# Four more seven-product pairs in three early groups of a hybrid attention and convolution block, and a later first one in the output product

## The chip, the cores and the metric

The kernel runs on one NeuronCore of a Trainium2 chip. The metric is the device time of one execution in microseconds. The engines are named as the profile names them: PE (TensorE, the matmuls), PEld (its weight loads), DVE (VectorE), ACT (ScalarE), POOL (GpSimd) and SP (SyncE, which issues the transfers).

## The reference, cut to what matters

One layer on 256 rows of 4096 numbers, everything in float32 (sizes: T = 256, D = 4096, the attention and the convolution half 2048 each):

```python
xn   = rms_norm(x, norm_in_g)
proj = xn @ w_in                       # 4096 x 14336
q, k, v, z_a, a_c, g_c, z_c = split(proj, 2048 each)
y_a  = rms_norm(chunked_attention(q, k, v), attn_out_g) * silu(z_a)
u    = a_c * sigmoid(g_c)              # "glu"
u    = causal_depthwise_conv(u, 31 taps) + b_dw
u    = silu(layer_norm(u))
y_c  = rms_norm(u @ w_pw + b_pw, conv_out_g) * silu(z_c)
h    = x + concat(y_a, y_c) @ w_out    # 4096 x 4096
gate = sigmoid(rms_norm(h) @ w_ple_gate + b)
h    = h + gate * (p @ w_ple)
out  = rms_norm(h, final_g)
```

## The kernel before, in words

**Products in float32.** A float32 matrix is split into a high part (a cast by ACT, L203, tiles `wh` for weights and `uh` for sums of weights) and a low part (the difference, by DVE, L204, `wl` and `ul`). One product of a 128x128 block of activations with 128x512 weights is then three matmuls: high by high, low by high, high by low. All matmuls of the large products are issued in `add`, L367; `product`, for v alone, issues at L217.

**Groups.** `mixed_product` makes one group: two blocks of 512 columns for two halves of 128 rows, in four accumulator banks of PSUM. It runs over the 32 blocks of the contraction in 16 pairs. A plain pair is 8 block products, 24 matmuls. A pair marked with a star in the order lists (`units("1 3 5 7 0* ...")`) is made as one step of Strassen's method with seven block products, 21 matmuls. For it DVE adds weights first (`ua`, L423 and L424; `ub`, L427 and L428), which are split too (two `uh` casts, two `ul` differences), and only half of the first weight tile is split. It uses four more banks, the helpers P1, P5, P6 and P7, which come from the pool `ps_tmp` of four banks that attention, transposes and the layer norm use as well, and which are read out behind the last seven-product pair of a group (`helper_sums`, L465 to L468). It also needs four combinations of the pair's blocks of activations: differences and sums with a high and a low part (`combine_again` and `combined_parts`, L279, L256 to L259 and, for the low part, L265). For x they lie in `xS`; there are combinations for the pairs 0, 2, 4 and 6, and so only these can be starred in the groups that read x early. Later the kernel has room for all even pairs.

**The order of the groups**, with the start of each group's matmuls in the profiled execution: glu(0) 6 us, glu(1) 99, q and k of heads(0) 186, its v 272, glu(2) 317, heads(1) 408 and v 496, glu(3) 542, heads(2) 633 and v, heads(3) 766 and v 859, the pointwise product 905, four gated z groups 999, four w_out groups 1328, the gate of the per-layer inputs 1666 to 2004. The attention of the heads of one call runs inside the next group: attention(1) in glu(3), attention(2) in heads(3).

**Work in between.** What isn't a product waits in a queue `later`: the 31 taps of the convolution (L666, L670), combinations, and, in heads(3), the layer norm: sums over channels, the mean as a matmul (L728), centring (L740), squares (L744, L748), variance, spread. `fill` takes a few from it behind each pair, four in these groups. A scheduler then sets the order of every engine's instructions; DVE, ACT and PE each run theirs strictly in that order. The mean matmul takes a bank of `ps_tmp`, so it stands behind the read of the first helper.

**Buffers.** Weights come by transfers of 512 KB on SP's queue into five tiles `wt`; `wh` and `wl` have three tiles each, `ua`/`ub` two, `uh`/`ul` two, the activation pool `act` eight places (for x while it is read, the outputs of attention and of the convolution).

The order lists concerned are `early` (glu(1) to glu(3) and all heads), `late` (the first w_out group and the first gate group) and `dense` (most later groups).

Of the kernel before, what the change touches and what calls it, by code (L numbers as in the profile page):

```python
# [16 lines left out]
P = 128  # L17
# [8 lines left out]
def hybrid_block(  # L26
# [285 lines left out]
    def units(text):  # L312

        return [(int(u.rstrip("*")), u.endswith("*")) for u in text.split()]


    dense = units("1 0* 3 2* 5 4* 6* 7 8* 9 10* 11 12* 14* 13 15")
    delayed = units("1 3 5 7 0* 9 2* 11 4* 13 6* 15 8* 10 12 14")
    first = units("0 1 3 5 7 9 11 13 15 2* 8 4* 10 6* 12 14")
    early = units("1 3 5 7 0* 9 2* 11 4* 13 6* 15 8 10 12 14")  # L320
    final = units("1 0* 3 2* 5 4* 6* 7 8* 9 10* 12* 11 13 14 15")
    late = units("1 3 5 7 9 11 13 15 0* 2 4* 6 8* 10* 12 14")

    def mixed_product(
        w, col, lhs, comb, order, on_helpers, ahead=None, fills=(0,), on_begin=None, apart=NB,
# [66 lines left out]
        for n, (pair, seven) in enumerate(order):  # L392
            if n < done:
                continue
            if ahead:
                ahead(pair)
            wts = []
            for k in range(2):
                wt = wpool.tile([P, 2, NB], F32, tag="w", name="wt")
                nc.sync.dma_start(wt, two_columns(w, 2 * pair + k, col, apart))  # L400
                wts.append(wt)
            if n >= len(order) - n_left:
                for k in range(2):
                    tiles = left[2 * (n - len(order) + n_left) + k]
                    held.append((2 * pair + k, parts_of(wts[k], 2, tiles and tiles())[0]))
                fill(fills[n % len(fills)])
                continue
            if not seven:
                for k in range(2):
                    add_plain(n, k, *parts_of(wts[k], 2)[0])  # L410
                fill(fills[n % len(fills)])
                continue
            begins = not helper
            if begins:
                for name in ("P1", "P5", "P7", "P6"):
                    helper[name] = ps_tmp.tile([P, NB], F32, tag="tmp", name=f"acc_{name}")
                banks.update(helper)
            w0, w1 = wts
            ua = upool.tile([P, 2, NB], F32, tag="u", name="ua")
            ub = upool.tile([P, 2, NB], F32, tag="u", name="ub")  # L420
            plus = partial(nc.vector.tensor_tensor, op=ALU.add)
            w0h, w0l = parts_of(w0, 1)[0]
            plus(ua[:, 0], w0[:, 0], w0[:, 1])  # L423
            plus(ua[:, 1], w0[:, 1], w1[:, 1])  # L424
            uah, ual = pair_parts(ua)
            w1h, w1l = parts_of(w1, 2)[0]
            plus(ub[:, 0], ua[:, 0], w1[:, 1])  # L427
            plus(ub[:, 1], ub[:, 0], w1[:, 0])  # L428
            ubh, ubl = pair_parts(ub)
            first = len(made)  # L430

            def s_of(i):
                t, at = comb[pair // 4], pair % 4
# [72 lines left out]
    ssq_x = cpool.tile([P, NH, D // NB], F32, name="ssq_x")  # L506
    xT = []

    xS = [big_tile(upool) for _ in range(2)]
    r_x = cpool.tile([P, NH], F32, name="r_x")  # L510

    def combinations(c, then=lambda ins: None):

        rest = []

        def begin():
            rows = spool.tile([P, 2, NB], F32, tag="stage", name="comb")
            rest.append(
                combine_again(
                    xS[c // 2], 2 * (c % 2), xT[c], 0, (rows[:, 0], rows[:, 1]), then  # L520
                )
            )

        return begin, lambda: rest.pop()()
# [150 lines left out]
    def glu_conv(c):  # L675
        if c == 0:
            sg, gate = scaled_pair(
                w_in0, o_a, o_g - o_a, first, r_x, (1,), begin=first_pairs
            )
        else:  # L680
            sg, gate = scaled_pair(w_in0, o_a + c * NB, o_g - o_a, early, r_x, (4,))
        for h in range(NH):
            nc.scalar.activation(gate[:, h, :], gate[:, h, :], AF.Sigmoid)
            tt(sg[:, h, :], sg[:, h, :], gate[:, h, :], ALU.mult)
        uT = spool.tile([P, 4, T], F32, tag="hd", name="uT", bufs=5)
        for pair in range(2):
# [178 lines left out]
    def heads(g):  # L865
# [9 lines left out]
            ),  # L875
        )
        nc.gpsimd.memset(bias[: P // 2, :, : P // 2], NEG)
        q, k = scaled_pair(w_in0, o_q + g * NB, o_k - o_q, early, r_x, (4,))
        qT, kT = to_heads(q, "qT"), to_heads(k, "kT")
        if g == n_g - 1:  # L880
            first_sums.close()
# [111 lines left out]
    for c0 in range(0, D // NB, 2):  # L993
# [8 lines left out]
        def on_helpers(helper):  # L1002
# [6 lines left out]
            tt(h11, h11, z[1][1], ALU.subtract)  # L1009

        acc = mixed_product(
            w_out[0], c0 * NB, yT, yS, dense if c0 else late, on_helpers,
            ahead=y_ahead if c0 == 0 else before_last(h_ahead) if c0 + 2 == D // NB else None,
            fills=(2,),
        )
# [203 lines left out]
```

## Time and profile before

| | |
|---|---|
| runs | 2042.84, 2042.05, 2042.83 us, median 2042.83 |
| profiled execution | 2042.15 us, of it 2040.4 span |
| PE busy | 2022.8 us, 99% of the span |
| DVE busy | 1879.8 us, 92% |
| ACT busy | 1177.1 us, 58% |
| granted clock | 0.998 |
| transfers | 412 MB, 202 GB/s |

The span runs from the first to the last instruction. "Busy" counts instructions of the engine itself. In a line of waits stand the waiting engine, the tile and line that waited, what ended the wait, and the total, the count and the longest in us. In a timeline stand start and duration in us, then the instruction with its shape; an "x3" row runs from the first one's start to the last one's end.

### The profile page before, as it was taken

How to read it: one execution, taken by the hardware profiler on the slowest of the kernel's cores; microseconds unless marked ns; L12 is line 12 of the kernel's file. 1: busy time of each engine (PE TensorE's matmuls, PEld its weight loads, DVE VectorE, ACT ScalarE, POOL GpSimd, SP SyncE). 2: the span in 40 equal slices, each digit the busy share in tenths (PEclk: the TensorE clock that was granted, in tenths of full speed). 3: DMA queues.
4: the chain of work that ended last, by engine and by line, in shares of the span. 5: the costliest groups of instructions: out<-in, count | busy, mean ns of one | idle time of the engine just before them, and what ended most of it. 6: DMA issues, size and time to landing. Idle time of an engine off the chain costs nothing.

```text
span 2040.4 us, 25991 instructions
## 1 busy us (share of the span) xinstructions
PE 2022.8 (99%) x9118; PEld 1662.6 (81%) x9118; DVE 1879.8 (92%) x2675; ACT 1177.1 (58%) x1517; POOL 15.7 (1%) x19
## 2 busy tenths in 40 slices
PE   9999999999999999999999999999999999999997
PEld 7888888887888788888888888888888888888876
DVE  7999999899877998866999999999999999999997
ACT  7655535554464536565566556676565666655555
POOL 0000000000000000000100000000000000000000
PEclk9999999999999999999999999999999999999999
DMA  8666665666566665555666666676666656666765
GB/s 290 191 196 207 196 197 165 205 190 194 175 196 200 194 187 184 182 189 196 198 209 204 196 216 201 221 231 207 212 204 200 215 185 207 197 223 205 233 209 176
DMA packets 161852, 412.28 MB, mean 202 GB/s; under 512 B 12974, under 2 KB 16190, under 8 KB 161722
## 3 DMA queue, kind: packets, MB, share of 16 engines
q1 hardware_dynamic: 161072, 409.80, 63.4%
q8 instruction: 71, 1.16, 0.2%
q10 hardware_dynamic: 650, 0.84, 0.1%
q14 instruction: 59, 0.48, 0.1%
HBM read 406.39 MB, written 4.19 MB: 201 GB/s over the span
## 4 chain that ended last, share of the span: by engine, by line
PE 91%; DVE 6%; issue 2%; ACT 0%; DMA 0%; POOLq 0%; POOL 0%; ACTq 0%; DVEq 0%
PE acc L367 64%; PE acc_P L367 15%; PE acc L217 9%; DVE wl L204 2%; DVE cv L670 2%; PE tmp_ps L169 1%; DVE ul L204 1%; PE tmp_ps L831 0%; PE tmp_ps L849 0%; PE tmp_ps L816 0%; DMA wt<-in_w_ple_dram 0%; PE tmp_ps L124 0%; PE tmp_ps L854 0%; PE tmp_ps L855 0%; PE tmp_ps L856 0%
## 5 line engine op out<-in xcount | busy, mean ns | idle before, releaser
L367 PE MATMUL acc<-wh,big_t 128*128 128x512 f32 x3874 | 1200.0, 392 | 0.0
L203 ACT CAST wh<-wt 128x1024 fp32r<-128x1024 f32 (+1 forms) x737 | 717.2, 982 | 584.4 <-PE acc L367 364.8
L204 DVE TENSOR_TENSOR wl<-wt,wh 128x1024 fp32r<-128x1024 f32 (+1 forms) x737 | 826.3, 1132 | 76.0 <-ACT wh L203 71.8
L367 PEld LDWEIGHTS acc<-wh,big_t 128*128 128x128 f32 x3874 | 724.9, 188 | 149.6 <-ACT big_t L155 0.6
L367 PE MATMUL acc<-wl,big_t 128*128 128x512 f32 x1937 | 746.6, 391 | 1.2 <-DVE wl L204 1.2
L367 PEld LDWEIGHTS acc<-wl,big_t 128*128 128x128 f32 x1937 | 363.1, 188 | 80.0 <-DVE wl L204 5.2
L670 DVE SCALAR_TENSOR_TENSOR cv<-uT,dw,cv 128x255 f32<-128x255 f32 (+25 forms) x480 | 203.5, 461 | 0.9
L203 ACT CAST uh<-ub 128x1024 fp32r<-128x1024 f32 x118 | 124.1, 1052 | 119.5 <-DVE ub L428 101.3
L367 PE MATMUL acc_P<-uh,big_t 128*128 128x512 f32 x594 | 181.4, 391 | 0.0
L217 PE MATMUL acc<-wh,big_t 128*128 128x512 f32 x560 | 173.3, 390 | 0.0
L203 ACT CAST uh<-ua 128x1024 fp32r<-128x1024 f32 x118 | 124.3, 1053 | 68.1 <-DVE ua L424 62.4
L204 DVE TENSOR_TENSOR ul<-ub,uh 128x1024 fp32r<-128x1024 f32 x118 | 143.8, 1219 | 8.2 <-ACT uh L203 7.6
L204 DVE TENSOR_TENSOR ul<-ua,uh 128x1024 fp32r<-128x1024 f32 x118 | 143.7, 1218 | 0.2
L367 PEld LDWEIGHTS acc_P<-uh,big_t 128*128 128x128 f32 x594 | 110.2, 188 | 25.8 <-ACT uh L203 3.8
L217 PEld LDWEIGHTS acc<-wh,big_t 128*128 128x128 f32 x560 | 105.0, 188 | 21.5
L367 PE MATMUL acc_P<-ul,big_t 128*128 128x512 f32 x297 | 113.9, 393 | 1.1 <-DVE ul L204 1.1
L217 PE MATMUL acc<-wl,big_t 128*128 128x512 f32 x280 | 109.0, 389 | 0.0
L423 DVE TENSOR_TENSOR ua<-wt 128x512 f32<-128x512 f32 x118 | 80.9, 685 | 20.9 <-DMA wt<-in_w_in_dram 14.9
L424 DVE TENSOR_TENSOR ua<-wt 128x512 f32<-128x512 f32 x118 | 80.7, 684 | 3.7 <-DMA wt<-in_w_in_dram 3.3
L428 DVE TENSOR_TENSOR ub<-ub,wt 128x512 f32<-128x512 f32 x118 | 80.8, 685 | 1.1
L427 DVE TENSOR_TENSOR ub<-ua,wt 128x512 f32<-128x512 f32 x118 | 80.6, 683 | 0.2
L367 PE MATMUL acc<-uh,big_t 128*128 128x512 f32 x236 | 73.4, 390 | 0.0
(213 smaller groups left out, 1398.2 us busy)
## 6 DMA issues: line engine op xcount, KB each, us to landing
wt<-in_w_in_dram SPq DMA_DIRECT2D x447, 512.0 KB, 4.0
wt<-in_w_out_dram SPq DMA_DIRECT2D x128, 512.0 KB, 4.2
wt<-in_w_ple_gate_dram SPq DMA_DIRECT2D x128, 512.0 KB, 4.1
wt<-in_w_pw_dram SPq DMA_DIRECT2D x32, 512.0 KB, 4.6
hc<-in_x_dram SPq DMA_DIRECT2D x8, 512.0 KB, 5.5
wt<-in_w_ple_dram SPq DMA_DIRECT2D x8, 512.0 KB, 4.7
xin<-in_x_dram SPq DMA_DIRECT2D x7, 512.0 KB, 8.1
out_dram<-hc SPq DMA_DIRECT2D x12, 256.0 KB, 2.5
```

The source lines that it names most:

```text
L169: nc.tensor.transpose(pt[:, i * T + h * P : i * T + (h + 1) * P], src[:, h, b * P : (b + 1) * P], ident,)
L203: nc.scalar.copy(wh[:, :kc, :], wt[:, :kc, :]),
L204: nc.vector.tensor_tensor(wl[:, :kc, :], wt[:, :kc, :], wh[:, :kc, :].bitcast(F32), ALU.subtract),
L217: nc.tensor.matmul(acc, a, b[:, k, :], start=kb == 0 and kind == 0, stop=kb == kblocks - 1 and kind == 2,)
L367: nc.tensor.matmul(banks[name], a, b, start=name not in begun, stop=final and ends[name] == n and kind == 2 and not (left and name in "P2 ...
L423: plus(ua[:, 0], w0[:, 0], w0[:, 1])
L424: plus(ua[:, 1], w0[:, 1], w1[:, 1])
L427: plus(ub[:, 0], ua[:, 0], w1[:, 1])
L428: plus(ub[:, 1], ub[:, 0], w1[:, 0])
L670: nc.vector.scalar_tensor_tensor(cv[:, i, PAD - k :], uT[:, i, : T + k - PAD], dw[:, b, k : k + 1], cv[:, i, PAD - k :], ALU.mult, ALU.add,)
```

## The change

`xS` becomes a dictionary by pair. Two more combinations are made: of pair 8 at the beginning of glu(2), of pair 10 at the beginning of glu(3). They go ahead of everything else in `later`, and into two places of the `act` pool that are free in those groups. The lists of the early groups then differ by group: glu(1), heads(0), heads(1) and heads(2) keep the old one; glu(2) and heads(3) make pair 8 as a seven-product pair too; glu(3) makes 8 and 10, and begins with its first starred pair at place 3 instead of 4. That is 4 more seven-product pairs, and 12 matmuls fewer. The first w_out group stars the same pairs 0, 4, 8 and 10 as before, but has pair 2 ahead of the first starred one, and only pair 14 behind the last. `delayed` was not used. The transfers' order on SP's queue and POOL's order don't change. Line numbers rise by 4 to 9: L367 is now L371, the centring L749, the helper sums L469 to L472.

```diff
+    early = {
+        4: units("1 3 5 7 0* 9 2* 11 4* 13 6* 15 8 10 12 14"),
+        5: units("1 3 5 7 0* 9 2* 11 4* 13 6* 15 8* 10 12 14"),
+        6: units("1 3 5 0* 7 2* 9 4* 11 6* 13 8* 15 10* 12 14"),
+    }
-    early = units("1 3 5 7 0* 9 2* 11 4* 13 6* 15 8 10 12 14")
     late = units("1 3 5 7 9 11 13 15 0* 2 4* 6 8* 10* 12 14")
+    later_still = units("1 3 5 7 9 11 13 15 2 0* 6 4* 12 8* 10* 14")
...
-    xS = [big_tile(upool) for _ in range(2)]
+    xS = {}
+    for c in range(0, 4, 2):
+        t = big_tile(upool)
+        xS.update({2 * c: (t, 0), 2 * c + 2: (t, 2)})
...
-            sg, gate = scaled_pair(w_in0, o_a + c * NB, o_g - o_a, early, r_x, (4,))
+            if c > 1:
+
+                xS[2 * c + 4] = act.tile([P, 2, 2, T], F32R, tag="act", name="comb_x"), 0
+                later.extendleft(reversed(combinations(c + 2)))
+            sg, gate = scaled_pair(w_in0, o_a + c * NB, o_g - o_a, early[3 + c], r_x, (4,))
...
-        q, k = scaled_pair(w_in0, o_q + g * NB, o_k - o_q, early, r_x, (4,))
+        q, k = scaled_pair(w_in0, o_q + g * NB, o_k - o_q, early[5 if g == n_g - 1 else 4], r_x, (4,))
...
-            w_out[0], c0 * NB, yT, yS, dense if c0 else late, on_helpers,
+            w_out[0], c0 * NB, yT, yS, dense if c0 else later_still, on_helpers,
```

Two places show what this does to DVE's order. The first is in heads(3), before, from the two splits of pair 15 (`wl_7200`, `wl_7216`) to the first split of pair 8 (`wl_7242`); `cv` are the convolution's tiles that are centred by the mean `mu`, `z` the helper sums, which come after the last starred pair, 6:

```order
L204 TENSOR_TENSOR wl_7216<-wt_7197,wh_7215 128x1024
L740 TENSOR_TENSOR cv_1025<-cv_1025,mu_7091 128x256 x3
L465 TENSOR_TENSOR z_7179<-acc_P6_6861,z_7179 128x512
L740 TENSOR_TENSOR cv_1025<-cv_1025,mu_7091 128x256
L466 TENSOR_TENSOR z_7180<-acc_P5_6859,z_7179 128x512
L740 TENSOR_TENSOR cv_1750<-cv_1750,mu_7091 128x256
L467 TENSOR_TENSOR z_7179<-acc_P7_6860,z_7179 128x512
L740 TENSOR_TENSOR cv_1750<-cv_1750,mu_7091 128x256
L468 TENSOR_TENSOR z_7180<-acc_P5_6859,z_7179 128x512
L740 TENSOR_TENSOR cv_1750<-cv_1750,mu_7091 128x256 x2
L740 TENSOR_TENSOR cv_3641<-cv_3641,mu_7091 128x256
L204 TENSOR_TENSOR wl_7242<-wt_7237,wh_7241 128x1024
```

Of the changed kernel the end of the same stretch on DVE, from the ninth centring to the first split of pair 12 (`wl_7386`). The last split ahead of it is the second of pair 10, and eight centrings of `cv_1025` and `cv_1750` stand between that and the first row:

```order
L749 TENSOR_TENSOR cv_3659<-cv_3659,mu_7142 128x256
L469 TENSOR_TENSOR z_7324<-acc_P6_6912,z_7324 128x512
L749 TENSOR_TENSOR cv_3659<-cv_3659,mu_7142 128x256
L757 TENSOR_TENSOR sq_7231<-sq_7231,sq_7273 128x1024
L470 TENSOR_TENSOR z_7325<-acc_P5_6910,z_7324 128x512
L749 TENSOR_TENSOR cv_3659<-cv_3659,mu_7142 128x256
L471 TENSOR_TENSOR z_7324<-acc_P7_6911,z_7324 128x512
L749 TENSOR_TENSOR cv_3659<-cv_3659,mu_7142 128x256
L472 TENSOR_TENSOR z_7325<-acc_P5_6910,z_7324 128x512
L749 TENSOR_TENSOR cv_5571<-cv_5571,mu_7142 128x256 x3
L757 TENSOR_TENSOR sq_7231<-sq_7231,sq_7338 128x1024
L749 TENSOR_TENSOR cv_5571<-cv_5571,mu_7142 128x256
```

The next row is that split. So nine centrings and four sums stood in one piece between two splits before; now it is 16 centrings, four sums and two additions of squares, and they stand two plain pairs from the group's end instead of four.

The second place is DVE in the first w_out group, around the first starred pair, 0. Before, from the split of half its first tile (`wl_11919`) to the first full split of its second round; `ul_11925` and `ul_11935` are the low parts of its two sums, `comb` the last combination of y:

```order
L204 TENSOR_TENSOR wl_11919<-wt_11908,wh_11918 128x512
L259 SCALAR_TENSOR_TENSOR comb_11819<-tmp_ps_11809,prm_122,comb_11819 128x128
L424 TENSOR_TENSOR ua_11916<-wt_11908,wt_11910 128x512
L427 TENSOR_TENSOR ub_11917<-ua_11916,wt_11910 128x512
L265 TENSOR_TENSOR comb_t_11744<-comb_11819,comb_t_11744 128x2x256
L204 TENSOR_TENSOR ul_11925<-ua_11916,uh_11924 128x1024
L204 TENSOR_TENSOR wl_11929<-wt_11910,wh_11928 128x1024
L428 TENSOR_TENSOR ub_11917<-ub_11917,wt_11910 128x512
L423 TENSOR_TENSOR ua_11999<-wt_11995 128x512
L204 TENSOR_TENSOR wl_11964<-wt_11959,wh_11963 128x1024
L204 TENSOR_TENSOR ul_11935<-ub_11917,uh_11934 128x1024
```

Now, with the plain pair 2 (`wl_11975`, `wl_11991`) ahead of it:

```order
L428 TENSOR_TENSOR ua_12014<-wt_12006,wt_12008 128x512
L259 SCALAR_TENSOR_TENSOR comb_11881<-tmp_ps_11871,prm_122,comb_11881 128x128
L204 TENSOR_TENSOR wl_11975<-wt_11970,wh_11974 128x1024
L204 TENSOR_TENSOR ul_12023<-ua_12014,uh_12022 128x1024
L265 TENSOR_TENSOR comb_t_11806<-comb_11881,comb_t_11806 128x2x256
L204 TENSOR_TENSOR wl_11991<-wt_11972,wh_11990 128x1024
L431 TENSOR_TENSOR ub_12015<-ua_12014,wt_12008 128x512
L204 TENSOR_TENSOR wl_12017<-wt_12006,wh_12016 128x512
L432 TENSOR_TENSOR ub_12015<-ub_12015,wt_12008 128x512
L204 TENSOR_TENSOR ul_12033<-ub_12015,uh_12032 128x1024
L204 TENSOR_TENSOR wl_12027<-wt_12008,wh_12026 128x1024
```

The sums and both low parts of pair 0 now stand among the splits of a plain pair, and the second low part no longer has a sum of the next starred pair and another pair's split directly ahead of it.

More of the change, by code (lines that the diff above doesn't have):

```diff
@@ L317, in hybrid_block @@
     dense = units("1 0* 3 2* 5 4* 6* 7 8* 9 10* 11 12* 14* 13 15")
-    delayed = units("1 3 5 7 0* 9 2* 11 4* 13 6* 15 8* 10 12 14")
     first = units("0 1 3 5 7 9 11 13 15 2* 8 4* 10 6* 12 14")
-    early = units("1 3 5 7 0* 9 2* 11 4* 13 6* 15 8 10 12 14")
+    early = {
[3 more added lines that the diff above has]
+    }
     final = units("1 0* 3 2* 5 4* 6* 7 8* 9 10* 12* 11 13 14 15")
     late = units("1 3 5 7 9 11 13 15 0* 2 4* 6 8* 10* 12 14")
+    later_still = units("1 3 5 7 9 11 13 15 2 0* 6 4* 12 8* 10* 14")
     def mixed_product(
@@ L432, in s_of @@
             def s_of(i):
-                t, at = comb[pair // 4], pair % 4
+                t, at = comb[pair] if isinstance(comb, dict) else (comb[pair // 4], pair % 4)
                 return [t[:, at + i // 2, q, (i % 2) * P : (i % 2 + 1) * P] for q in range(2)]
@@ L518, in begin @@
             rest.append(
-                combine_again(
-                    xS[c // 2], 2 * (c % 2), xT[c], 0, (rows[:, 0], rows[:, 1]), then
-                )
+                combine_again(*xS[2 * c], xT[c], 0, (rows[:, 0], rows[:, 1]), then)
             )
```

## The prediction, made before the changed kernel was run

> **What bounds the kernel now.** I read the page's first and fourth parts first, then what PE waits for, then stretch by stretch the groups that the diff names.
>
> ```profile
> PE 2022.8 (99%) x9118; PEld 1662.6 (81%) x9118; DVE 1879.8 (92%) x2675; ACT 1177.1 (58%) x1517; POOL 15.7 (1%) x19
> PE 91%; DVE 6%; issue 2%; ACT 0%; DMA 0%; POOLq 0%; POOL 0%; ACTq 0%; DVEq 0%
> ```
>
> PE is busy for 2022.8 of 2040.4 us, and the chain that ended last is PE for 91% and DVE for 6%. DVE, at 92%, is the engine from which the added work takes room. The next view is all that PE waits for, in the whole span.
>
> ```profile
> PE acc L367 <- DVE wl L204: 1.2, 3, 0.6
> PE tmp_ps L124 <- DVE ssq_f L1027: 1.2, 1, 1.2
> PE acc_P L367 <- DVE ul L204: 1.1, 2, 0.9
> PE tmp_ps L816 <- DVE z L489: 0.5, 2, 0.3
> ```
>
> These are four lines of total, count and longest. Apart from the program's first instruction, PE waits 2.8 us in seven waits, always for DVE. So a matmul fewer is worth its pace, unless DVE falls behind. The stretches are, in this order, glu(2), the q and k products of heads(1), glu(3), those of heads(3), and the first w_out group. Below them is a stretch with only the products' own line, which gives that pace.
>
> ```profile
> core 0: us, PE busy (x) PEld busy (x) DVE busy (x) ACT busy (x) POOL busy (x), PEclk, DMA share, GB/s
> 317.05:408.38 91.33, 91.33 (x423) 75.00 (x422) 82.39 (x135) 51.56 (x76) 0.00 (x0) 1.00 0.61 185
> 408.38:495.50 87.12, 86.49 (x381) 70.11 (x379) 84.91 (x134) 45.47 (x51) 0.31 (x1) 1.00 0.64 195
> 542.40:633.34 90.94, 90.94 (x422) 75.01 (x421) 65.27 (x86) 51.55 (x76) 0.00 (x0) 1.00 0.61 185
> 766.39:858.50 92.11, 92.11 (x428) 75.87 (x427) 78.60 (x115) 55.16 (x80) 1.01 (x2) 1.00 0.60 187
> 1327.51:1418.63 91.12, 90.26 (x422) 74.62 (x420) 87.30 (x136) 59.23 (x86) 0.00 (x0) 1.00 0.69 218
> ```
>
> ```profile
> 1418.63:1500.23 81.60, 81.60 (x362) 67.57 (x360) 1.00 0.63 207
> ```
>
> DVE stands idle for 91.33 − 82.39 = 8.9 us in glu(2), 2.2 in heads(1), 25.7 in glu(3), 13.5 in heads(3) and 3.8 in the w_out group. One matmul is 81.60 / 360 = 0.2267 us.
>
> **The change part by part.** *Matmuls.* A plain pair is 24 matmuls and a seven-product pair 21, so four more of the latter remove 12: 12 × 0.2267 = **−2.72 us**, all on the path, since PE is busy throughout the three groups.
>
> The Trainium skill, in "TensorE: Matmul & The Clock Gate", section "Back-to-back issue gap", gives about 131 ns as the sustained spacing of 512-column matmuls in a stream with weight loads; by it the 12 would be worth only 1.57 us, an estimate. The row above says 227 ns for this stream, and the row decides.
>
> *What DVE gets for it.* These are rows of the page's fifth part and, last, the groups of a combination's five operations (the lines of the program that make S).
>
> ```profile
> L204 DVE TENSOR_TENSOR wl<-wt,wh 128x1024 fp32r<-128x1024 f32 (+1 forms) x737 | 826.3, 1132 | 76.0 <-ACT wh L203 71.8
> L204 DVE TENSOR_TENSOR ul<-ub,uh 128x1024 fp32r<-128x1024 f32 x118 | 143.8, 1219 | 8.2 <-ACT uh L203 7.6
> L423 DVE TENSOR_TENSOR ua<-wt 128x512 f32<-128x512 f32 x118 | 80.9, 685 | 20.9 <-DMA wt<-in_w_in_dram 14.9
> L279 DVE TENSOR_TENSOR comb<-big_t x12: 682/685/694, 27.9 to 992.9; 128x512 f32<-128x512 f32 x12
> L256 DVE TENSOR_TENSOR comb<-comb x28: 277/284/293, 28.6 to 1708.8; 128x128 f32<-128x128 f32 x28
> L265 DVE TENSOR_TENSOR big_t<-comb,big_t x22: 678/684/694, 35.2 to 1698.6; 128x512 fp32r<-128x512 f32 x22
> ```
>
> A seven-product pair adds four sums of 0.685 and two splits of 1.219, and halves one of the two splits of weights (about −0.5): 4.7 us. A combination is 0.685 + 4 × 0.284 + 0.684 = 2.5 us. The ACT part (for a pair two casts more, the row below) is covered: ACT is idle for over a third of every one of these stretches.
>
> ```profile
> L203 ACT CAST uh<-ua 128x1024 fp32r<-128x1024 f32 x118 | 124.3, 1053 | 68.1 <-DVE ua L424 62.4
> ```
>
> *glu(2)*: one pair and one combination, 7.2 us, and PE is 0.68 us shorter: 7.9 of 8.9 idle us. The combination begins before the group's first products. So **0**, covered by DVE's idle time alone, with a rest of 1 us; if that cover is gone, what is left over goes to heads(1), where DVE has 2.2 us of rest, and from there to PE (a rival below).
>
> *glu(3)*: two pairs and one combination, 11.9 us, against 25.7 idle. But the first seven comes one place earlier, at place 3, while the four heads of attention(1) still run, so that their chain (matmul, softmax rows on DVE and ACT, transpose, matmul) is laced into less plain work. No row shows that mix. The nearest are the seven waits above: none at all at one end, two of the longest (0.9) at the other; I take two of the mean, 2.8 / 7 = 0.4 each, less a little: **+0.6** (0 to 1.8). In the steady alternation the balance is exact:
>
> ```profile
> L204 DVE TENSOR_TENSOR ul<-ub,uh x3: 1216/1219/1222, 353.2 to 373.6; 128x1024 fp32r<-128x1024 f32 x3
> ```
>
> Two rounds of a seven and a plain pair take DVE 20.4 us in glu(2), with about four convolution taps in each; PE needs 2 × 45 × 0.2267 = 20.4. A longer row of sevens therefore eats no lead by itself.
>
> *heads(3)*: one pair, 4.7 us plus 0.68, of 13.5. Here the place matters. The layer norm's mean matmul (L728) takes the first helper bank when the last seven has been read from it, and everything of the norm hangs on that. First DVE around it, then two pieces of PE.
>
> ```profile
> 828.52 1.23 DVE L204 TENSOR_TENSOR wl<-wt,wh 128x1024 fp32r<-128x1024 f32 x1 [0.78 <-ACT wh L203]
> 829.66 1.09 DVE L740 TENSOR_TENSOR cv<-cv,mu 128x256 f32<-128x256 f32 x3
> 830.67 0.68 DVE L465 TENSOR_TENSOR z<-acc_P,z 128x512 f32<-128x512 f32 x1
> 831.27 0.42 DVE L740 TENSOR_TENSOR cv<-cv,mu 128x256 f32<-128x256 f32 x1
> ...
> 834.07 1.08 DVE L740 TENSOR_TENSOR cv<-cv,mu 128x256 f32<-128x256 f32 x3
> 835.08 2.35 DVE L204 TENSOR_TENSOR wl<-wt,wh 128x1024 fp32r<-128x1024 f32 x2
> 837.35 1.21 DVE L748 TENSOR_TENSOR sq<-sq 128x1024 f32<-128x1024 f32 x1
> 838.48 1.08 DVE L740 TENSOR_TENSOR cv<-cv,mu 128x256 f32<-128x256 f32 x3
> ```
>
> ```profile
> 827.60 0.70 PE L728 MATMUL tmp_ps<-lnsum,mean_w 128*128 128x256 f32 x2
> ```
>
> ```profile
> 836.34 0.62 PE L367 MATMUL acc<-wh,big_t 128*128 128x512 f32 x2
> 836.79 0.39 PE L367 MATMUL acc<-wl,big_t 128*128 128x512 f32 x1
> ```
>
> Before, nine centrings and the four helper sums stand between two splits of weights: the next split ends at 835.08 + 1.14 = 836.2, PE reads it at 836.79: 0.5 us to spare. Now the last seven is pair 8, 45 matmuls (10.20 us) behind pair 6, and only three plain pairs follow. DVE's order then puts all 16 centrings, the four sums and two additions of squares ahead of the first split of pair 12. By the starts above a centring takes 0.337 (1.01 / 3), a sum 0.60, an addition 1.13: 16 × 0.337 + 4 × 0.60 + 2 × 1.13 = 10.05 us. They begin at 829.66 + 10.20 = 839.86, the split follows at 849.91 and ends at 851.05. PE reaches pair 12 as long after the mean matmul as it now reaches pair 8, at 836.34 + 10.20 = 846.54, and its order does eight matmuls with the high part first (1.81 us): 848.35. PE is held for 851.1 − 848.35 = **+2.75 us**. The low end is 0, if DVE gets to the centrings earlier or PE comes later; it can't be a gain. The high end is 4.25: an addition of squares that waits for its ACT square as long as DVE's longest wait for an ACT cast in glu(3) (1.5, quoted under C). After that each split comes about when PE wants it: late next are the variance and its spread, which end with the group, at 0.
>
> *First w_out group.* Same sevens, the first a plain pair later. Before, PE is held there:
>
> ```profile
> 1380.29 0.39 PE L367 MATMUL acc_P<-uh,big_t 128*128 128x512 f32 x1
> 1381.54 0.50 PE L367 MATMUL acc_P<-ul,big_t 128*128 128x512 f32 x1 [0.86 <-DVE ul L204]
> ```
>
> The two starts are 1.25 apart instead of 0.227: **−1.02** when ul stands in DVE's order ahead of what it now follows and PE asks for it 5.4 us later. It can't be more than that. In return only pair 14 follows the last seven where 12 and 14 did, so the evacuations of the helper banks come later against the next group's first plain pair. The wait is not seen before; its ends are 0 and the 0.9 of the longest wait, and I take **+0.2**, since DVE is 24 matmuls later there but its order has the same rows.
>
> Sum: −2.72 + 0 + 0.6 + 2.75 − 1.02 + 0.2 = **−0.2 us** against the profiled execution (2042.15 us, with a span of 2040.4). The median of the runs, 2042.83, lies 0.68 above it and the runs reach from 2042.05 to 2042.84; half of that is added: 2042.15 − 0.2 + 0.35 = **2042.3 us**.
>
> **The rivals.** Within 0.2% (4.1 us, about what a measurement of this kernel can tell from no change) means 2038.7 to 2046.9.
>
> A: *the norm doesn't hold PE.* DVE has 13.5 us of rest in heads(3), and PE has not one wait there now; against it stands the spare time of 0.5. Then 2042.3 − 2.75 = 2039.6. Only with glu(3) free of waits too, −3.74 in all, does it come to 2038.4 to 2039.1, on the bound of faster.
>
> B: *glu(2)'s cover fails.* DVE's 8.9 idle us are partly waits for ACT's casts and for PE, not room at will; if those recur, the 7.2 us aren't taken up there, and heads(1), with 2.2 us of rest and PE waits of its own, hands the rest on one to one:
>
> ```profile
> PE acc L367 <- DVE wl L204: 0.6, 2, 0.4
> ```
>
> (all that PE waits for in 408.4 to 495.5). It decides from about 4.6 us left over; with up to 7 the time is 2047 to 2049: slower. Against it: the waits stand early in the group and its end has plain pairs.
>
> C: *the weights come late in glu(3).* There are five tiles of weights, and a seven holds two of them while four sums read them; DVE waits at the sums in glu(3) now, and a transfer lands 4.0 us after its issue:
>
> ```profile
> DVE wl L204 <- ACT wh L203: 16.0, 14, 1.5
> DVE ua L423 <- DMA wt<-in_w_in_dram: 4.7, 3, 1.8
> ```
>
> ```profile
> wt<-in_w_in_dram SPq DMA_DIRECT2D x447, 512.0 KB, 4.0
> ```
>
> The three waits passed PE by so far; one of their mean for each added pair and none covered would be 2 × 1.6 = 3.2 at the most, about +1 with what PE has in hand: 2043.3.
>
> D: *the hold slows the clock.* No stretch shows it: PEclk is 1.00 everywhere, and the longest wait within the products is 0.9 us. At the program's start the first five matmuls take 0.45 each:
>
> ```profile
> 1.18 2.32 PE L124 MATMUL tmp_ps<-idle 128*128 128x512 bf16 x5 [1.18 <-DVE ssq_f L1027]
> ```
>
> If PE fell back to that pace for some 5 us after a hold of 2.75 to 4.25 us, half of those would be lost: +2.5, 2044.8. This is the rule of the Trainium skill, "TensorE: Matmul & The Clock Gate", section "Part 1: The HAM clock gate", which halves the clock after an idle window of about 3.4 us.
>
> **How the numbers follow.** The forecast has 0.53, A 0.25 (0.10 of it below 2038.7), B 0.14, C 0.05, D 0.03. Faster: 0.10 and 0.02 for luck elsewhere, 0.12. Slower: B and 0.02 of C and D together, 0.16. Same: 0.72. The range takes in A's 2039.6 with its free glu(3) down to 2038.9; above it the forecast's own high ends (glu(3) 1.2 more, the norm 1.5, the w_out group 0.7: 2045.7) and part of D: 2046.5.
>
> **What would show it.** In the changed profile: 12 matmuls fewer over the three groups, at 0.227 each; in heads(3) a PE wait of about 2.7 us for wl some 10 us after the mean matmul, behind the centrings on DVE; no wait for ul at the w_out group's first seven; in glu(3) one to three waits under 1 us; none more in heads(1). A heads(3) without that wait, or waits of several us in heads(1), would make the forecast wrong.

## The result, and the profile after

The changed kernel takes 2046.32 us in the median of 22 runs (2042.83 to 2049.6), the kernel before 2042.69 us in the median of 22 (2040.69 to 2045.03). The ratio is 1.0018, with a 95% interval of 1.0011 to 1.0024: 3.6 us slower. That is inside the predicted range and within 0.2%, but it is a loss that the runs tell from no change, where the forecast, 2042.3 us, was a zero sum. The profiled execution took 2047.33 us, a microsecond over its median, with a span of 2045.5.

First the busy times, then all that PE waits for in the changed kernel (total, count, longest).

```profile
PE 2023.7 (99%) x9106; PEld 1660.4 (81%) x9106; DVE 1900.1 (93%) x2711; ACT 1183.8 (58%) x1527; POOL 15.7 (1%) x19
```

```profile
PE acc L371 <- DVE wl L204: 4.1, 4, 2.8
PE tmp_ps L825 <- DVE z L493: 1.5, 2, 1.1
PE tmp_ps L124 <- DVE ssq_f L1036: 1.2, 1, 1.2
PE tmp_ps L863 <- DVE pT L860: 0.8, 1, 0.8
PE acc_P L371 <- ACT wh L203: 0.5, 1, 0.5
PE acc_P L371 <- DVE ul L204: 0.4, 1, 0.4
PE tmp_ps L858 <- ACT s L851: 0.3, 1, 0.3
```

PE has 12 matmuls fewer and yet 0.9 us more of busy time, and its waits have grown from 4.0 to 8.8 us. One of them is 2.8 us long. Where that lies is seen from a table of stretches, each from the first matmul of a group to the first of the next: glu(2), glu(3), heads(3) with its v, and the first two w_out groups together.

```profile
core 0: us, PE busy (x) PEld busy (x) DVE busy (x) ACT busy (x) POOL busy (x), PEclk, DMA share, GB/s
316.70:407.41 90.71, 90.66 (x419) 74.53 (x418) 88.43 (x146) 53.60 (x79) 0.00 (x0) 1.00 0.61 186
542.50:634.28 91.78, 90.69 (x416) 73.64 (x415) 74.19 (x100) 54.58 (x81) 0.00 (x0) 1.00 0.59 183
767.45:909.78 142.33, 139.49 (x642) 115.01 (x640) 117.39 (x175) 88.66 (x134) 1.01 (x2) 0.99 0.59 181
1332.49:1505.45 172.96, 172.40 (x782) 141.99 (x781) 165.24 (x228) 108.13 (x143) 0.00 (x0) 1.00 0.66 213
```

Of the kernel before, the first two are quoted in the prediction (91.33 and 90.94); the same two last ones are these:

```profile
766.39:904.76 138.37, 138.37 (x644) 114.56 (x643) 113.01 (x169) 86.65 (x132) 1.01 (x2) 1.00 0.60 186
1327.51:1500.23 172.72, 171.86 (x782) 142.19 (x780) 165.67 (x228) 107.98 (x143) 0.00 (x0) 1.00 0.66 213
```

So glu(2) is 0.62 us shorter, glu(3) 0.84 longer with six matmuls fewer, heads(3) 3.96 longer with three fewer, and the w_out groups 0.24 longer. The rest of the profile's difference is mostly heads(1), 1.1 us longer, and the last w_out group, 0.9 longer; the experiments come back to both. The lines of heads(3), DVE and then PE, around the place that the prediction named:

```profile
840.89 3.10 DVE L749 TENSOR_TENSOR cv<-cv,mu 128x256 f32<-128x256 f32 x9
843.90 0.68 DVE L469 TENSOR_TENSOR z<-acc_P,z 128x512 f32<-128x512 f32 x1
...
849.60 1.23 DVE L757 TENSOR_TENSOR sq<-sq 128x1024 f32<-128x1024 f32 x1
850.74 0.42 DVE L749 TENSOR_TENSOR cv<-cv,mu 128x256 f32<-128x256 f32 x1
851.08 2.35 DVE L204 TENSOR_TENSOR wl<-wt,wh 128x1024 fp32r<-128x1024 f32 x2
```

```profile
852.35 2.08 PE L371 MATMUL acc<-wl,big_t 128*128 128x512 f32 x4 [2.84 <-DVE wl L204]
854.23 1.05 PE L371 MATMUL acc<-wh,big_t 128*128 128x512 f32 x2
855.08 0.63 PE L371 MATMUL acc<-wl,big_t 128*128 128x512 f32 x1
855.51 0.70 PE L371 MATMUL acc<-wh,big_t 128*128 128x512 f32 x2
856.05 0.40 PE L371 MATMUL acc<-wl,big_t 128*128 128x512 f32 x1
856.28 0.62 PE L371 MATMUL acc<-wh,big_t 128*128 128x512 f32 x2
```

DVE works from 840.89 to 851.08 on centrings, sums and squares: 10.19 us, where the prediction counted 10.05. PE stands for 2.84 us. And then the matmuls themselves are slow: from 852.35 to 855.51 seven of them (4 + 2 + 1) take 3.16 us, 0.45 each instead of 0.227; the single row from 855.08 to the next start at 855.51 is 0.43. The clock that the profile recorded as granted (the column PEclk, the third number from the end) is at half for 3.41 us there, and at full speed on both sides:

```profile
848.84:852.25 3.41, 0.68 (x3) 0.21 (x2) 3.35 (x7) 2.95 (x4) 0.00 (x0) 1.00 0.00 0
852.25:855.66 3.41, 3.31 (x8) 2.63 (x9) 3.41 (x5) 1.10 (x2) 0.00 (x0) 0.50 0.57 166
855.66:859.07 3.41, 3.41 (x17) 2.77 (x16) 2.42 (x5) 1.05 (x1) 0.00 (x0) 1.00 0.91 289
```

In glu(3) the new wait looks like this, DVE first:

```profile
561.75 0.68 DVE L427 TENSOR_TENSOR ua<-wt 128x512 f32<-128x512 f32 x1
562.56 0.17 DVE L855 RECIPROCAL den<-den 128x2 f32<-128x2 f32 x1
563.83 0.69 DVE L428 TENSOR_TENSOR ua<-wt 128x512 f32<-128x512 f32 x1 [1.10 <-DMA wt<-in_w_in_dram]
564.44 0.55 DVE L860 COPY pT<-tmp_ps 128x384 f32<-128x384 f32 x1
```

```profile
565.05 0.49 PE L863 MATMUL tmp_ps<-v,pT 128*128 128x128 f32 x2 [0.78 <-DVE pT L860]
```

A sum of the next seven stands ahead of attention's copy in DVE's order and waits 1.10 us for its weights; the copy waits behind it, and PE for the copy.

### The profile page after: what moved, and what is told of

Its sections match the earlier page's. It is cut to its first block, busy times and chain, and to the rows that moved or that the text cites. A ratio compares the mean times of both kernels' runs of the same rounds, so it can differ in the third digit from the quotient of the medians.

```text
span 2045.5 us, 26026 instructions
## 1 busy us (share of the span) xinstructions
PE 2023.7 (99%) x9106; PEld 1660.4 (81%) x9106; DVE 1900.1 (93%) x2711; ACT 1183.8 (58%) x1527; POOL 15.7 (1%) x19
## 4 chain that ended last, share of the span: by engine, by line
PE 87%; DVE 9%; issue 2%; DMA 1%; ACT 1%; POOLq 0%; POOL 0%; ACTq 0%; DVEq 0%
PE acc L371 63%; PE acc_P L371 15%; PE acc L217 6%; DVE wl L204 4%; DVE cv L675 3%; PE tmp_ps L169 1%; DMA wt<-in_w_in_dram 1%; DVE ul L204 1%; DMA wt<-in_w_out_dram 0%; ACT wh L203 0%; PE tmp_ps L825 0%; PE tmp_ps L858 0%; PE tmp_ps L840 0%; ACT uh L203 0%; PE acc L359 0%
## 5 line engine op out<-in xcount | busy, mean ns | idle before, releaser
L371 PE MATMUL acc<-wh,big_t 128*128 128x512 f32 x3818 | 1183.3, 392 | 0.0
L371 PEld LDWEIGHTS acc<-wh,big_t 128*128 128x128 f32 x3818 | 714.6, 188 | 147.5 <-ACT big_t L155 0.6
L371 PE MATMUL acc<-wl,big_t 128*128 128x512 f32 x1909 | 736.6, 392 | 4.2 <-DVE wl L204 4.1
L371 PEld LDWEIGHTS acc<-wl,big_t 128*128 128x128 f32 x1909 | 358.4, 188 | 83.7 <-DVE wl L204 9.7
L675 DVE SCALAR_TENSOR_TENSOR cv<-uT,dw,cv 128x255 f32<-128x255 f32 (+23 forms) x480 | 204.1, 463 | 0.9
L371 PE MATMUL acc_P<-uh,big_t 128*128 128x512 f32 x594 | 181.7, 392 | 0.1
L217 PE MATMUL acc<-wh,big_t 128*128 128x512 f32 x560 | 173.4, 390 | 0.0
L203 ACT CAST uh<-ua 128x1024 fp32r<-128x1024 f32 x122 | 128.5, 1053 | 75.5 <-DVE ua L428 69.5
L204 DVE TENSOR_TENSOR ul<-ub,uh 128x1024 fp32r<-128x1024 f32 x122 | 148.9, 1220 | 7.9 <-ACT uh L203 6.8
L204 DVE TENSOR_TENSOR ul<-ua,uh 128x1024 fp32r<-128x1024 f32 x122 | 148.8, 1219 | 0.3
L371 PEld LDWEIGHTS acc_P<-uh,big_t 128*128 128x128 f32 x594 | 110.0, 188 | 26.2 <-ACT uh L203 4.5
L217 PEld LDWEIGHTS acc<-wh,big_t 128*128 128x128 f32 x560 | 105.0, 188 | 21.7
L371 PE MATMUL acc_P<-ul,big_t 128*128 128x512 f32 x297 | 114.0, 394 | 0.6 <-DVE ul L204 0.4
L427 DVE TENSOR_TENSOR ua<-wt 128x512 f32<-128x512 f32 x122 | 83.8, 687 | 28.4 <-DMA wt<-in_w_in_dram 19.3
L217 PE MATMUL acc<-wl,big_t 128*128 128x512 f32 x280 | 108.9, 389 | 0.0
L428 DVE TENSOR_TENSOR ua<-wt 128x512 f32<-128x512 f32 x122 | 83.6, 686 | 4.7 <-DMA wt<-in_w_in_dram 3.6
L371 PE MATMUL acc_P<-wh,big_t 128*128 128x512 f32 x244 | 75.4, 390 | 0.5 <-ACT wh L203 0.5
```

The lines of the kernel that those rows point to most:

```text
L203: nc.scalar.copy(wh[:, :kc, :], wt[:, :kc, :]),
L204: nc.vector.tensor_tensor(wl[:, :kc, :], wt[:, :kc, :], wh[:, :kc, :].bitcast(F32), ALU.subtract),
L217: nc.tensor.matmul(acc, a, b[:, k, :], start=kb == 0 and kind == 0, stop=kb == kblocks - 1 and kind == 2,)
L371: nc.tensor.matmul(banks[name], a, b, start=name not in begun, stop=final and ends[name] == n and kind == 2 and not (left and name in "P2 ...
L675: nc.vector.scalar_tensor_tensor(cv[:, i, PAD - k :], uT[:, i, : T + k - PAD], dw[:, b, k : k + 1], cv[:, i, PAD - k :], ALU.mult, ALU.add,)
```

## The experiments

All start from the changed kernel, unless the text says otherwise. Medians are of 11 runs beside 15 to 33 of the kernel before on the same chip; the intervals are some 0.09% wide on either side, nearly 2 us, so what is worth less than that is read from the traces. The kernel before itself has a median of 2042.34, 2041.93 or 2042.21 us in these batches, 2042.69 in the one of the result. So the distance from the kernel before in the same batch is what is compared; for the changed kernel it was +3.6 us.

**heads(3) with the old list.**

```diff
-        q, k = scaled_pair(..., early[5 if g == n_g - 1 else 4], r_x, (4,))
+        q, k = scaled_pair(..., early[4], r_x, (4,))
```

> Only heads(3) goes back to the old list (pair 8 plain there); the rest is as in the changed kernel. In the changed kernel's trace heads(3) holds PE for 2.84 us of idle time (two matmuls start 3.22 apart) and then nine matmuls start 0.43 apart instead of 0.227. Theory (the norm's place in DVE's order holds PE, and the hold is long enough to slow PE's clock): both go, 3.0 + 1.7, and 0.68 for three matmuls comes back, about 4.0 us faster than the changed kernel, near 2042.3; DVE's order in heads(3) is again the one of the kernel before, with no PE wait there. Rival (the slow matmuls have another cause, such as weights landing late near 853 us): only 3.0 - 0.68 = 2.3 us faster, near 2044, and the slow matmuls stay. Rival (heads(3) is only where a delay from glu(2) and glu(3) comes out): a wait of PE of 2 to 3 us appears in heads(3) or v3 all the same.

Measured: 2043.03 us, ratio 1.0004 (0.9995 to 1.0012), which is 0.7 us above the kernel before. The stretch of heads(3) is the one of before again, without a PE wait:

```profile
766.18:904.57 138.39, 138.39 (x645) 114.49 (x643) 113.09 (x169) 86.67 (x132) 1.01 (x2) 1.00 0.60 186
```

So this one star carries most of the loss (the distance falls from 3.6 to 0.7 us): the stretch is 3.94 us shorter without it (142.33 − 138.39), with three matmuls more. That is 3.94 + 0.68 = 4.62 us of hold and slow matmuls, against the 4.7 of the theory.

**Small matmuls inside the hold.** `idle` is moved to the pool that lives through the kernel, and the mean's bank is kept under a name; then

```diff
+        def heat():
+            for _ in range(22):
+                nc.tensor.matmul(st["m"][:, T:], idle[:, :P], idle[:, :T], start=True, stop=True)
...
             later.append(partial(square, c))
+            if c == 3:
+                later.append(heat)
```

> The changed kernel with 22 small matmuls on zeros (128x256, bf16, into an unused half of the mean's bank) placed in PE's order inside the hold of heads(3), between the eight matmuls of the high part and the first of the low part of pair 12. They feed no result. DVE's order is the same. Theory (an idle PE of 2.84 us loses its clock): PE is no longer idle for long there, and the matmuls after the hold start 0.227 apart: about 1.7 us faster than the changed kernel, near 2044.6; the hold itself stays at about 3 us. Rival (the slow matmuls wait for something else: weights, PSUM, DVE): they stay 0.43 apart and the time stays at 2046.3, or rises by what of the 22 matmuls sticks out (22 x 0.11 = 2.4 us, at most a few tenths).

```profile
846.55 1.98 PE L371 MATMUL acc<-wh,big_t 128*128 128x512 f32 x8
848.37 2.58 PE L753 MATMUL tmp_ps<-idle 128*128 128x256 bf16 x22
851.36 1.21 PE L371 MATMUL acc<-wl,big_t 128*128 128x512 f32 x4 [0.42 <-DVE wl L204]
852.41 0.62 PE L371 MATMUL acc<-wh,big_t 128*128 128x512 f32 x2
852.87 0.39 PE L371 MATMUL acc<-wl,big_t 128*128 128x512 f32 x1
```

The hold is as long as ever, from the end of the eight matmuls to 851.36, but behind it the matmuls run at their pace at once (four from 851.36 to 852.41, 0.26 each, and two at 0.23). The stretch of heads(3) takes 140.79 us here, 1.54 less than 142.33. The granted clock is 1.00 from 848.3 to 857.6 us in this profile, and DVE's order is the one of the changed kernel until well behind the hold. The slow matmuls are thus a consequence of PE's idleness, and not of late weights or of DVE. The median, 2046.02 (ratio 1.0016, 1.0007 to 1.0025), is 3.7 us above the kernel before, no better than the changed kernel; the interval holds the expected 2044.6 as well, so the times alone neither confirm the 1.7 us nor exclude them.

**Six small matmuls instead of 22** leave PE idle for 2.2 us.

> The changed kernel with 6 instead of 22 small matmuls inside the hold of heads(3), about 0.65 us of work, so that PE is idle for 2.2 us behind them instead of 2.84. Theory (it is the unbroken idle time that slows the clock, and between the 1.2 us that passed without it and 2.84 there is a bound): either the matmuls after the hold start 0.227 apart, and the bound lies between 2.2 and 2.84, or 0.43 apart, and it lies between 1.2 and 2.2. Rival (any hold there slows them whatever PE does, with 22 matmuls only by chance not): 0.43 apart, and nothing can be said of the bound.

```profile
852.88 1.20 PE L371 MATMUL acc<-wl,big_t 128*128 128x512 f32 x4 [2.17 <-DVE wl L204]
853.91 0.74 PE L371 MATMUL acc<-wh,big_t 128*128 128x512 f32 x2
854.45 0.63 PE L371 MATMUL acc<-wl,big_t 128*128 128x512 f32 x1
854.88 1.05 PE L371 MATMUL acc<-wh,big_t 128*128 128x512 f32 x2
```

2.17 us of idle time slow it too: five matmuls at full pace, one in between, then seven at 0.43. The granted clock is 0.50 from 854.25 to 857.66. The single time was 2047.46.

**Both kernels a second time.**

> The kernel before, for a second profile. Theory (heads(1) and the first w_out group vary between executions by a microsecond, as the profiles of the variants suggest): q and k of heads(1) with v1 take 133 to 134 us from start to start, and the first w_out group's wait for ul is anything from 0.3 to 0.9. Rival (the first profile's values are the kernel's own): 134.0 and 0.86 again.

> The changed kernel, for a second profile. Theory: glu(3) and heads(3) take 91.6 and 142.4 us from start to start again, 0.7 and 4.0 more than before, with the wait of 2.84 us and slow matmuls behind it; heads(1) with v1 takes about 133 instead of 135.1, and the last w_out group 83.4 instead of 84.3. Rival: 135.1 and 84.3 again, and so losses of the change.

The single times were 2041.34 and 2048.7. Of the kernel before, heads(1) with v1 takes 133.41 us (134.02 the first time), and the wait for ul in the first w_out group is 0.68 (0.86). Of the changed kernel, glu(3) and heads(3) repeat within 0.03, 91.77 and 142.36, heads(1) with v1 takes 133.94 (135.09) and the last w_out group 84.03 (84.33). So heads(1)'s microsecond wasn't the change's. The last w_out group is 0.6 us longer than before (83.40 in both profiles) here too, nearer the rival than the theory; in the ten profiles of variants it takes 83.40 to 83.79, and what lengthens it stayed open. In heads(2), which the change leaves as it was, PE waits once for 1.75 us, which the first profile hasn't. Two variants have such a wait of 1.1 to 1.2 us and neither profile of the kernel before has one; whether the change causes it isn't shown. That idle time of 1.75 us did not slow the matmuls behind it:

```profile
669.78 0.50 PE L371 MATMUL acc_P<-ul,big_t 128*128 128x512 f32 x1 [1.75 <-DVE ul L204]
670.11 0.62 PE L371 MATMUL acc_P<-uh,big_t 128*128 128x512 f32 x2
670.58 0.40 PE L371 MATMUL acc_P<-ul,big_t 128*128 128x512 f32 x1
```

**The centrings one pair later.**

```diff
         later.append(lambda: mean(st["s"]))
-        later.extend(rest)
+        later.extend(rest * 2)
```

> The changed kernel, with four empty entries more in the queue of deferred work behind the mean, so that the centrings are taken one pair later. In DVE's order 12 centrings, four sums and one addition then stand ahead of the first low part of pair 12 instead of 16, four and two, 2.5 us less, and the last four centrings stand behind both low parts of pair 12. Theory: the hold shrinks from 2.84 us idle to 0.3 to 0.6, is too short to slow the clock, and the time falls by 2.5 + 1.7 = 4.2 us, to about 2042; the three matmuls saved in heads(3) are then kept. Rival (the end of the norm is what holds, not its middle): as much comes back at v or at the pointwise product, and the time stays over 2045.

Measured: 2043.69 us, ratio 1.0007 (0.9998 to 1.0016). PE's idle time at pair 12 is 0.40 us, and the matmuls behind it are not slow:

```profile
848.43 1.20 PE L371 MATMUL acc<-wl,big_t 128*128 128x512 f32 x4 [0.40 <-DVE wl L204]
849.47 1.77 PE L371 MATMUL acc<-wh,big_t 128*128 128x512 f32 x7
```

The stretch of heads(3) takes 139.26 us: 3.07 less than in the changed kernel, but 0.89 more than before the change with three matmuls fewer. The rival's part is thus about 1.6 us: waits of some tenths for splits, and for the evacuations that now share DVE with the end of the norm, at the change to v.

**glu(3) with the old list** (`early[5 if c == 2 else 4]`, and no combination of pair 10).

> Only glu(3) goes back to the old list, without the combination of pair 10; glu(2), heads(3) and the w_out group are as in the changed kernel, so the long wait in heads(3) stays. Matmul starts of glu(3) in the changed kernel's trace are late by 3.28 us in all (start to start less 0.227, of gaps over 0.3), 1.48 in the kernel before: two waits at attention (for pT 0.8, for the softmax 0.3) and some splits that come just in time. Theory (the two added pairs cost more in waits than their six matmuls save): glu(3)'s waits go, 1.8 us less, 1.36 us for six matmuls come back: 0.4 us faster than the changed kernel, near 2045.9, which only the trace can show; the trace has no wait over 0.3 us in glu(3). Rival (the prediction's price, 0.6 of waits for 1.36 gained): 0.8 us slower, near 2047.1.

Measured: 2045.6 us, ratio 1.002 (1.0011 to 1.0029). PE has no wait in glu(3), which takes 90.99 us, 0.8 less than in the changed kernel with six matmuls more. As the theory had it, the two pairs cost more than they save in the profiles of the changed kernel; the times, 3.7 us above the kernel before against 3.6, can't tell. The size varies: in the eight profiles with glu(3) as in the changed kernel, the group takes 90.90 to 92.39 us, four times 91.7 to 91.8, where the kernel before has 90.94 and 90.97. In seven of them the waits cost more than the 1.36 us that six matmuls save, in one (90.90) about as much.

**glu(3) with its six sevens, but the first at place 4.**

```diff
-        6: units("1 3 5 0* 7 2* 9 4* 11 6* 13 8* 15 10* 12 14"),
+        6: units("1 3 5 7 0* 9 2* 11 4* 13 6* 15 8* 10* 12 14"),
```

> As the changed kernel, but glu(3) begins its seven-product pairs at place 4, as before (1 3 5 7 0* 9 2* 11 4* 13 6* 15 8* 10* 12 14), with the same six of them. Theory (it is the first seven among the last of attention's heads that makes PE wait, not the number of sevens): the waits for pT and the softmax in glu(3), 1.3 us over the kernel before, go, and the time falls by 1 to 1.4 us, near 2045.1; glu(3) is then 0.6 to 1.2 us shorter than in the kernel before. Rival (the number of sevens: DVE's lead is used up toward the group's end): waits for wl behind pair 8 and 10 come in their place, and the time stays at 2046.3 or rises.

Measured: 2044.24 us, ratio 1.0011 (1.0002 to 1.002), which is 2.3 us above the kernel before, 1.3 less than the changed kernel. PE has no wait in this stretch:

```profile
540.51:630.15 89.64, 89.64 (x417) 73.91 (x415) 74.22 (x100) 55.31 (x81) 0.00 (x0) 1.00 0.60 188
```

It is 2.14 us shorter than in the changed kernel, with the same matmuls, and 1.30 shorter than before: the six matmuls' 1.36, in full. The place of the first seven was the cost, not their number.

**glu(2) with the old list** (its combination is still made there).

> Only glu(2) goes back to the old list; the combination of pair 8 is still made there, for glu(3) and heads(3). Theory (DVE is the bound over glu(2) and heads(1) together, so three matmuls fewer in glu(2) only make PE wait later): the wait of 1.1 us for z at the start of v1 and the waits of 0.5 and 0.2 for wl in heads(1) shrink to those of the kernel before, and v1 starts no later than in the changed kernel, against the start of glu(2): 0 to 0.4 us faster, near 2046. Rival (glu(2) keeps its gain): 0.68 us slower, near 2047, and heads(1)'s waits stay.

Measured: 2045.7 us, ratio 1.0021 (1.0012 to 1.003). glu(2) takes 91.41 us and heads(1) with v1 133.42; in the nine profiles of the other variants and repeats that have the added seven, glu(2) takes 90.73 to 90.77 and heads(1) with v1 anything from 132.88 to 133.94. The theory tested here, that heads(1) hands glu(2)'s gain back, is wrong: glu(2) keeps its 0.6 us, and the wait for z at v1 stays without the seven too. That wait is 0.3 us at most in the two profiles of the kernel before and in the first of the two kernels put together below, which makes the combination of pair 8 in glu(3), and 0.8 to 1.2 in all others. So it seems to come with the combination in glu(2); heads(1) with v1 isn't longer for it (134.70 us where it is short).

**The first w_out group with the old list.**

```diff
-            w_out[0], c0 * NB, yT, yS, dense if c0 else later_still, on_helpers,
+            w_out[0], c0 * NB, yT, yS, dense if c0 else late, on_helpers,
```

> Only the first w_out group goes back to the list before; the early groups are as in the changed kernel. In the changed kernel's trace the wait for a low part of a sum (1.02 us) at that group's first starred pair is gone, but at the next group's start PE waits 0.5 us for an ACT cast and loses about 0.8, and some tenths more for low parts of sums in that group. Theory (the later start gives nothing net): the time is within 0.4 us of the changed kernel, 2046.3, with the wait of about 0.9 us for ul back and the wait for the cast gone. Rival (the prediction's term): 0.8 us slower than the changed kernel, near 2047.1.

Measured: 2046.16 us, ratio 1.0017 (1.0008 to 1.0026), 3.8 us above the kernel before and so, within what the runs tell, equal to the changed kernel. The two w_out groups take

```profile
1331.23:1503.43 172.20, 171.83 (x781) 142.22 (x780) 165.61 (x228) 108.11 (x143) 0.00 (x0) 1.00 0.66 213
```

172.20 us, 0.76 less than in the changed kernel. The wait for ul is 0.4 us here, where the two profiles of the kernel before have 0.86 and 0.68: that wait isn't a fixed cost. The wait for the cast at the next group's start, about 0.7 us of lost time, is in every profile with the new list and in none with the old. In the changed kernel's trace it is this one:

```profile
1422.21 0.39 PE L371 MATMUL acc<-wl,big_t 128*128 128x512 f32 x1
1423.12 0.73 PE L371 MATMUL acc_P<-wh,big_t 128*128 128x512 f32 x2 [0.53 <-ACT wh L203]
```

**What was left, put together, twice.** First with pair 8 a seven in heads(3) and the later centrings, and glu(2) as before; then with glu(2)'s seven and heads(3) as before. Both have six sevens in glu(3) from place 4 on, and the old w_out list.

> What the traces leave of the change, put together: glu(2) and the first w_out group as before, both new combinations made in glu(3), glu(3) with six seven-product pairs from place 4 on, heads(3) with pair 8 as a seven-product pair and the norm's centrings one pair later. Nine matmuls fewer than before, 2.04 us. Theory (the losses are those places and no others): 0.5 to 1.5 us faster than the kernel before, 2041 to 2042, with no PE wait over 0.6 us in glu(3) and heads(3). Rival (DVE has no room for more than the old sevens anywhere in these groups): not faster than the kernel before, waits for wl in glu(3) or heads(2).

> The changed kernel's new pairs where the traces show no loss: pair 8 in glu(2), pairs 8 and 10 in glu(3) with the first seven at place 4, heads(3) and the first w_out group as before the change. Nine matmuls fewer than before, 2.04 us. Theory (the losses came from heads(3)'s norm, from the early first seven in glu(3) and from the w_out list, nothing else): glu(2) is 0.6 us and glu(3) 1.3 us shorter than before, heads(3) as before, in all about 1.9 us faster than the kernel before, near 2040.5. Rival (heads(1) or heads(2) hand it back through DVE): those two are a microsecond longer together, and the time is that of the kernel before.

Measured: 2040.77 us, ratio 0.9995 (0.9987 to 1.0004), and 2040.75 us, ratio 0.9992 (0.9983 to 1.0001). Their medians are 1.2 and 1.5 us below that of the kernel before in the same batches, near what was expected; both intervals still touch 1. In the second one glu(2) takes 90.75 us, glu(3) 89.60 and heads(3) 138.35, as the theory has it, and against the kernel before it is 5.1 us better than the changed kernel (−1.5 against +3.6). That it beats the kernel before is likely by the traces and not shown by the times.

## Why the prediction was right and wrong

The forecast was a sum near zero, and the measured change is +3.6 us, the other way. That 2046.3 still lies in the range is owed to the width of its upper side and not to the forecast: three terms were too low by over a microsecond each, and none was too high. By its steps, with stretches of the profiles:

- *The matmuls*, −2.72 us: right. Where PE doesn't wait (glu(2), and glu(3) with the later start), three and six matmuls are worth 0.6 and 1.3 us, the 0.2267 of the row each. The 131 ns of the Trainium skill ("TensorE: Matmul & The Clock Gate", section "Back-to-back issue gap"), which the prediction set beside it, would give 0.4 and 0.8, an estimate; this stream doesn't have that pace.
- *glu(2)*, hidden: right. Rival B (its cover fails) didn't come about.
- *heads(3)*, the hold: right in place, mechanism and size. Predicted were +2.75 us behind 10.05 us of DVE work; measured, 2.84 us of idle time, 3.0 from start to start, behind 10.19.
- *What follows the hold*: this is the step that failed most. The sum has no term for it: once the split has come, PE was to go on at full pace. Rival D (a hold of this length slows the clock) was given 0.03, with the argument that PEclk is 1.00 everywhere. But nowhere in the trace of before does PE idle for more than 1.2 us, so the rows could not speak against it, and the forecast itself contained a hold of 2.75 us: D was not a rival to the forecast but a part of it. Its price was put at 2.5 us, for 5 us at half pace; the runs show 1.7, for 3.41 us. With the hold 0.25 longer from start to start, heads(3) came out 1.9 us over its terms.
- *glu(3)*, +0.6 of waits: mis-sized. They are 0.84 + 1.36 = 2.2 us, above the high end of 1.8, so this group missed by 1.6. The prediction took the mean of waits seen elsewhere. The trace showed what was needed: DVE waits for weights at `ua` in glu(3) (4.7 us in three waits), and whatever stands behind `ua` in DVE's order inherits that wait; before, nothing urgent stood there. Rival C had the transfer but not the copy of attention behind it. The wait traced to this is 0.78 us, another of 0.31 is for the softmax, and the rest is small delays that were not followed up one by one. Starting one place later removes 2.14 of the 2.2 us.
- *The w_out group*, −1.02 + 0.2: wrong by 1.1 us (−0.82 forecast, +0.24 measured). A wait of one profiled execution was taken for a fixed cost; with the same list it varies from none (in the second of the kernels put together) to 0.86 us. And the price of the later list is a wait for ACT's cast, 0.7 us in every profile, not the evacuations on DVE that were thought of. What makes that cast late was not tested; ACT itself stands idle for 0.71 us directly before it.

Together: −0.6 (glu(2)) + 0.84 + 3.96 + 0.24 = 4.4 us in the first pair of profiles, where the medians differ by 3.6; the difference is within what a single execution varies by. The three misses, 1.9, 1.6 and 1.1, make up the distance of 4.6 us between this sum and the forecast's −0.2.

## What to carry to other kernels

Work that hangs on a late event (here the layer norm behind the last read of a helper bank) is priced by where it lands in a strictly ordered queue: count the row of instructions ahead of the next operand and compare it with when the consumer comes. If a forecast contains a hold of PE as long as those that slowed the clock here (2.2 us and more), add the slower clock behind it to the same forecast, not to a rival. Before a seven-product step is put next to latency-bound work, see what stands behind its first use of fresh weights in the queue, since a wait for a transfer is passed on to all of that (here 1.10 us of DVE, and 0.78 us of PE behind it).

## What the runs showed of the hardware

The clock fell after shorter idle times than expected. In all six profiles with the hold of 2.83 to 2.84 us and no work inside it, and in the one with 2.17, the granted clock goes to 0.50 for 3.41 us. A matmul takes 0.43 us in it instead of 0.23, and 1.6 to 1.7 us are lost. The fall comes between 0.2 us before and 1.4 us after PE starts again; in the profile shown above it was 0.1 us before. An idle time of 1.75 us, seen once, and the many up to 1.2 us left the clock at 1.00.

The length of an idle time may not be all that counts. In each of the 14 profiles the changes of the granted clock lie whole multiples of 3.413 us apart; in the changed kernel's, for example, the clock rises at 5.74, falls at 852.25, which is 248 such steps later, and rises again one step on. So the clock seems to be set anew at fixed steps, and what decides is then how much PE worked within one step. In the step before the fall PE was busy for 0.68 of 3.41 us in the changed kernel and for 1.37 with the six small matmuls, and the clock fell; in the step that holds the whole wait of 1.75 us it was busy for 1.66, and the clock stayed. The first row is of the kernel with the six, the second of the changed kernel's second profile:

```profile
850.84:854.25 3.41, 1.37 (x6) 1.16 (x7) 3.41 (x5) 2.58 (x3) 0.00 (x0) 1.00 0.06 7
666.75:670.16 3.41, 1.66 (x8) 1.07 (x7) 3.41 (x5) 1.99 (x3) 0.00 (x0) 1.00 0.55 158
```

By this reading the bound lay between 1.37 and 1.66 us of work in a step, or 1.75 and 2.03 us of idle time, by one observation on either side. No run was made to place a wait differently against the steps. That the share within a step decides, and not the unbroken idle time (with a bound between 1.75 and 2.17 us), is therefore read from the traces and not tested. The Trainium skill, in "TensorE: Matmul & The Clock Gate", section "Part 1: The HAM clock gate", speaks of an idle window of about 3.4 us; the measured idle times that were enough are shorter than that, and the half pace and the 3.41 us agree with it.
